# A list schedule of one decoder layer with 112 of its 758 groups of tasks at another rank

## The chip, the cores and the metric

One NeuronCore of a Trainium2 chip. The metric is the device time of one execution in microseconds (us). Every time in this document is that of the device or of the hardware profiler's trace.

## What is computed

One layer of a hybrid decoder on 512 tokens of width 1024, in float32. The reference, cut to what matters here:

```python
ada = c @ w_ada + b_ada                       # six vectors of 1024: sh1, sc1, gt1, sh2, sc2, gt2
h = rms_norm(x, norm1_w) * (1 + sc1) + sh1
proj = h @ w_in                               # 1024 x 10016
att_in, rwkv_in, gate_in = split(proj, ...)   # 4608, 3360, 2048 columns
y_att = attention_mixer(att_in) @ w_att_out   # 3 groups (window, dilation), 8 heads of 64
y_rwkv = rwkv7_mixer(rwkv_in, ...) @ w_rwkv_out   # 16 heads of 64, low-rank decay, a and gate
g_att, g_rwkv = split(sigmoid(gate_in + b_gate))
x = x + gt1 * ((g_att * y_att + g_rwkv * y_rwkv) @ w_o)
h = rms_norm(x, norm2_w) * (1 + sc2) + sh2
x = x + gt2 * conv_ffn(h, w_up, conv_w, conv_b, w_down)   # gated, causal convolution of width 3
return rms_norm(x, norm_f_w)
```

## The kernel before

**Arithmetic.** A long product is made of three matmuls per 128 rows of the contraction: each float32 operand is split into a high part (`hi`, fp32r, by ScalarE) and a low part (`lo`, by VectorE), and hi\*hi, hi\*lo and lo\*hi are added up in one PSUM bank. So every weight block is loaded by a DMA from SP's queue, cast on ScalarE (`whi`, L1181), subtracted on VectorE (`wlo`, L1184) and used by TensorE 24 times (L148). Such a block with its product is a "body". The buffers are few: two raw weight blocks, two split ones, and two PSUM banks (`mm`) for the long products.

**Stages.** The start (conditioning): x is loaded, normed and turned; VectorE multiplies the rows of `w_ada` by c and adds them up in four rounds (L506 and L508), and each round gives two of the eight blocks of h. As the blocks come, the first products of the attention run: four accumulations `early` (e = 0 to 3, over k = 0 to 7) and the value products `v`. The fourth of the `early` ones and the value products sit in `mm` banks; `early` is copied out by ScalarE (e = 0, 1) and VectorE (e = 2, 3, L606). When all of the start is done, a point named `wide` frees its memory for the rest of the attention. Then the attention: the projections `qk00` to `qk12` (part, group), scores `sc`, `stat` (L825), `exp`, turns `pt` and `pts`, values `po`, and at the end the shares of the groups (`pa`, L1067). Then RWKV: three lora products (`lw`, and `lg` twice), and for each of eight pairs of heads the products k, r and v with their token shift. `shift` is one ScalarE instruction (L1192) and one on VectorE (L1194), and the second one releases the `mm` bank. Four groups of two pairs each get the inverse of a triangular matrix (VectorE steps, `inv0` to `inv3`) and a chain of eight steps (`xy`, `u`, `w`, `xo`). Products of the branch gates (`gate`, tile `pg`) fill TensorE beside the chains. At the end of RWKV the products with `w_att_out` (`pa`) and the first ones with `w_rwkv_out` (`pr`) begin.

**What sets the order.** All of this up to the first `pr` products is not written in its final order. `Layer` adds some thousands of tasks to a `Plan`: each has an engine (`PE`, `DVE`, `ACT`, `POOL` or `DMA`, which is SP's queue), an assumed time, a function that writes its instructions, tasks that it depends on, buffers that it takes and gives, and a rank `prio`. `Plan.run` plays through the tasks with the assumed times. Whenever an engine is free, it sorts its ready tasks by `(prio, uid)` and starts the first whose buffers are free. The order in which it starts them is the order of each engine's instructions in the program, and on the chip each engine's queue runs in that order, with semaphores between the queues. The assumed times set the order and nothing else. A lower rank goes first; at equal ranks the task that was added first goes first.

The ranks before follow a few constants: chains 0.0 (`C_`), what empties PSUM 1.0 (`E_`), small matmuls 1.0 and up (`S_`), weight loads and splits 2.0 plus the number of the body (`W_`), long matmuls 10.0 plus that number (`U_`), the preparation of pair m 200.0 + 0.1 m (`V_`), the inverses 200.25, 200.35, 200.65 and 200.75, and 220.0 for what has time (`M_`). The norms and gates of the chains of groups 0 to 2 have 150.0.

**Behind the plan** the rest is written out by hand: the other `pr` products, `w_o` (tile `o`), the up projections (`u`), the down projections (`o`) and the last norm. It begins at about 740 us of the profile.

The change touches one function, `Plan.run`, and adds a table beside it.

Of the kernel before, what the change touches and what calls it, by code (L numbers as in the profile page):

```python
# [43 lines left out]
        self.left, self.at, self.users, self.uid = 0, 0.0, [], 0  # L44


class Plan:


# [18 lines left out]
    def run(self):  # L68
        now, events, busy, open_ = 0.0, [], {}, {}
        room = self.room  # L70

        def push(at, kind, t):
            heapq.heappush(events, (at, kind, t.uid, t))

        for t in self.tasks:
            if not t.left:
                push(0.0, 1, t)
        done = 0
        while events:
            now = events[0][0]  # L80
            while events and events[0][0] <= now + 1e-9:
                _, kind, _, t = heapq.heappop(events)
                if kind == 1:
                    open_.setdefault(t.eng, []).append(t)
                    continue
                if kind == 0:
                    busy[t.eng] = False
                    if t.lag:
                        push(now + t.lag, 2, t)
                        continue  # L90
                for r in t.give:
                    room[r] += 1
                done += 1
                for u in t.users:
                    u.at = max(u.at, now + (self.HOP if u.eng != t.eng and "NO" not in (u.eng, t.eng) else 0.0))
                    u.left -= 1
                    if not u.left:
                        push(u.at, 1, u)
            for eng, ready in open_.items():
                if busy.get(eng):  # L100
                    continue
                ready.sort(key=lambda t: (t.prio, t.uid))
                for t in ready:
                    need = {r: t.take.count(r) for r in t.take}
                    if all(room[r] >= n for r, n in need.items()):
                        for r in t.take:
                            room[r] -= 1
                        ready.remove(t)
                        busy[eng] = True
                        t.fn()  # L110
                        push(now + t.us, 0, t)
                        break
        assert done == len(self.tasks), (now, room, [(t.eng, t.name or t.fn.__qualname__, t.take)
                                                     for r in open_.values() for t in r][:20])
# [2337 lines left out]
```

## Time and profile before

| | us |
|---|---|
| device time, three runs: median | 1192.46 |
| lowest and highest of them | 1192.05, 1192.62 |
| span of the profiled execution, first to last instruction | 1189.3 |
| TensorE busy in it (matmuls) | 1154.6 |
| VectorE busy | 741.6 |
| ScalarE busy | 542.4 |
| GpSimd busy | 130.6 |

The profiled execution is told by its span; 3.16 us lie between that span and the median of the three runs. TensorE shows as busy from the start of a matmul to its modelled end, and ends overlap the next start, so 512-column matmuls of 390 to 400 ns each follow each other every 0.23 us. The idle time before an instruction stands in square brackets in the timeline, with what released it. The DMA engines moved 138.93 MB. The mean granted clock of TensorE over the span is 0.994 of full speed.

### The profile page before, as it was taken

How to read it: one execution, taken by the hardware profiler on the slowest of the kernel's cores; microseconds unless marked ns; L12 is line 12 of the kernel's file. 1: busy time of each engine (PE TensorE's matmuls, PEld its weight loads, DVE VectorE, ACT ScalarE, POOL GpSimd, SP SyncE). 2: the span in 40 equal slices, each digit the busy share in tenths (PEclk: the TensorE clock that was granted, in tenths of full speed). 3: DMA queues.
4: the chain of work that ended last, by engine and by line, in shares of the span. 5: the costliest groups of instructions: out<-in, count | busy, mean ns of one | idle time of the engine just before them, and what ended most of it. 6: DMA issues, size and time to landing. Idle time of an engine off the chain costs nothing.

```text
span 1189.3 us, 19029 instructions
## 1 busy us (share of the span) xinstructions
PE 1154.6 (97%) x7440; PEld 928.5 (78%) x7440; DVE 741.6 (62%) x1250; ACT 542.4 (46%) x1012; POOL 130.6 (11%) x271
## 2 busy tenths in 40 slices
PE   4899999999999999999999999999999999999997
PEld 3788888788687876777787667788888888888886
DVE  6788864432778977756896655845665656562235
ACT  4475622523566374464545543534444444431223
POOL 4000000000300024131103231014000000000001
PEclk9899999999999999999999999999999999999999
DMA  9845873120233332322331626730333333333231
GB/s 315 269 125 168 260 246 108 56 79 1 74 111 89 93 107 85 107 81 85 89 94 48 197 68 190 207 129 19 89 100 95 96 100 94 101 106 106 89 124 71
DMA packets 168329, 138.93 MB, mean 117 GB/s; under 512 B 8785, under 2 KB 150187, under 8 KB 168239
## 3 DMA queue, kind: packets, MB, share of 16 engines
q1 hardware_dynamic: 168095, 137.45, 37.9%
q8 instruction: 58, 0.95, 0.3%
q14 instruction: 32, 0.26, 0.1%
q10 hardware_dynamic: 144, 0.26, 0.1%
HBM read 127.39 MB, written 10.30 MB: 116 GB/s over the span
## 4 chain that ended last, share of the span: by engine, by line
PE 87%; DVE 9%; issue 2%; ACT 1%; DMA 1%; SPq 0%; POOL 0%; POOLq 0%; DVEq 0%; ACTq 0%
PE u L148 22%; PE o L148 13%; PE qk L148 10%; PE v L148 9%; PE pg L148 7%; PE pr L148 3%; PE r L148 3%; PE k L148 3%; PE pa L148 2%; PE pt L151 2%; PE xy L148 2%; PE sc L148 2%; PE early L148 2%; PE po L148 1%; DVE acc L508 1%
## 5 line engine op out<-in xcount | busy, mean ns | idle before, releaser
L194 DVE TENSOR_TENSOR wlo<-raw,whi 128x1024 fp32r<-128x1024 f32 x65 | 79.6, 1225 | 132.9 <-ACT whi L193 132.9
L148 PE MATMUL u<-h2hi,whi 128*128 128x512 f32 (+2 forms) x368 | 140.6, 382 | 0.0
L148 PE MATMUL u<-h2lo,whi 128*128 128x512 f32 (+2 forms) x368 | 140.6, 382 | 0.0
L148 PE MATMUL u<-h2hi,wlo 128*128 128x512 f32 (+2 forms) x368 | 140.5, 382 | 0.0
L1181 ACT CAST whi<-raw 128x1024 fp32r<-128x1024 f32 (+2 forms) x73 | 72.6, 994 | 123.0 <-PE qk L148 47.1
L193 ACT CAST whi<-raw 128x1024 fp32r<-128x1024 f32 x65 | 68.5, 1054 | 90.5 <-PE o L148 53.7
L1184 DVE TENSOR_TENSOR wlo<-raw,whi 128x1024 fp32r<-128x1024 f32 (+2 forms) x73 | 83.8, 1148 | 25.2 <-ACT whi L1181 24.9
L148 PEld LDWEIGHTS u<-h2lo,whi 128*128 128x128 f32 x368 | 69.1, 188 | 13.3 <-POOL h2lo L405 0.2
L148 PEld LDWEIGHTS u<-h2hi,wlo 128*128 128x128 f32 x368 | 69.1, 188 | 13.2
L148 PEld LDWEIGHTS u<-h2hi,whi 128*128 128x128 f32 x368 | 69.1, 188 | 13.0
L2278 DVE SCALAR_TENSOR_TENSOR u<-u,cols,u 128x511 f32<-128x511 f32 x88 | 65.7, 746 | 4.3 <-ACT u L2276 2.7
L148 PE MATMUL qk<-hhi,wlo 128*128 128x512 f32 x160 | 64.0, 400 | 0.0
L148 PE MATMUL qk<-hhi,whi 128*128 128x512 f32 x160 | 63.9, 400 | 0.0
L148 PE MATMUL qk<-hlo,whi 128*128 128x512 f32 x160 | 63.4, 396 | 0.0
L148 PE MATMUL o<-whi,fhi 128*128 128x512 f32 x144 | 56.1, 390 | 0.3 <-DVE u L2278 0.3
L148 PE MATMUL o<-wlo,fhi 128*128 128x512 f32 x144 | 56.0, 389 | 0.0
L148 PE MATMUL o<-whi,flo 128*128 128x512 f32 x144 | 56.0, 389 | 0.0
L148 PE MATMUL pg<-hlo,whi 128*128 128x512 f32 x128 | 51.9, 406 | 0.0
L148 PE MATMUL pg<-hhi,wlo 128*128 128x512 f32 x128 | 51.9, 406 | 0.0
L148 PE MATMUL pg<-hhi,whi 128*128 128x512 f32 x128 | 51.4, 402 | 0.0
L825 DVE CUSTOM_DVE_ANT_0 sm<-sc,m 128x256 f32<-128x256 f32 (+1 forms) x64 | 23.9, 403 | 38.5 <-PE sc L148 37.0
L347 DVE SCALAR_TENSOR_TENSOR acc<-araw,cols,acc 128x1024 f32<-128x1024 f32 x28 | 35.9, 1281 | 12.4 <-DMA araw<-in_w_ada_dram 12.2
(457 smaller groups left out, 2755.3 us busy)
## 6 DMA issues: line engine op xcount, KB each, us to landing
raw<-in_w_in_dram SPq DMA_DIRECT2D x62, 512.0 KB
raw<-in_w_up_dram SPq DMA_DIRECT2D x44, 512.0 KB
araw<-in_w_ada_dram SPq DMA_DIRECT2D x32, 512.0 KB
raw<-in_w_down_dram SPq DMA_DIRECT2D x22, 512.0 KB
araw<-in_w_ada_dram SPq DMA_DIRECT2D x32, 256.0 KB
wvraw<-in_w_in_dram SPq DMA_DIRECT2D x20, 256.0 KB
raw<-in_w_rwkv_out_dram SPq DMA_DIRECT2D x8, 512.0 KB
raw<-in_w_o_dram SPq DMA_DIRECT2D x8, 512.0 KB
```

Of the source, the lines that this page charges most:

```text
L148: return self.nc.tensor.matmul(out, lhsT, rhs, start=start, stop=stop)
L151: self.nc.tensor.matmul(out, in_, self.ident[: in_.shape[0], : in_.shape[0]], is_transpose=True, start=start, stop=stop,)
L193: self.nc.scalar.copy(hl[0], raw)
L194: (lo_eng or self.nc.vector).tensor_tensor(hl[1], raw, hl[0], op=ALU.subtract)
L347: nc.vector.scalar_tensor_tensor(d["acc"], raw, ck, d["acc"], op0=ALU.mult, op1=ALU.add)
L508: nc.vector.scalar_tensor_tensor(a["acc"], a[k], ck, a["acc"], op0=ALU.mult, op1=ALU.add)
L825: nc.vector.tensor_tensor_reduce(d["sm", h][:, :wd], d["sc"][h][:, :wd], m[:, 256 - wd : 256] if gi == 0 else m[:, :wd], 1.0, 3.0e38, op0= ...
L1181: nc.scalar.copy(d["w"][0], d["raw"])
L1184: nc.vector.tensor_tensor(d["w"][1], d["raw"], d["w"][0], op=ALU.subtract)
L2278: nc.vector.scalar_tensor_tensor(u[:, d:], pu[:, : S - d], ch(c), u[:, d:], op0=ALU.mult, op1=ALU.add)
```

## The change

`Plan.run` adds a number to the rank of each task before it starts. The number is looked up in a table by the task's engine, its name, the name of its function and its old rank, rounded to six places; tasks that agree in all four are one group. 112 of the 758 groups stand in the table, and the others add 0. No task, buffer, tile, dependency or assumed time is changed, and neither is anything behind the plan. Most entries move a group from one of the bands above into another. The diff, with the entries that the prediction speaks of and some of the others:

```diff
+RANKS = {
...
+    ('ACT', '', '<lambda>', 200.75): -172.69,
+    ('ACT', '', 'r_hi', 200.1): -201.6,
+    ('ACT', 'k3 hi', 'hi', 50.0): 170.84,
+    ('ACT', 'lg hi', 'hi', 39.0): -39.96,
+    ('ACT', 'lg hi', 'hi', 40.0): -37.56,
...
+    ('ACT', 'r3 hi', 'hi', 51.0): 213.82,
...
+    ('ACT', 'shift', '<lambda>', 1.0): 44.79,
...
+    ('DMA', 'gate in', '<lambda>', 220.0): -160.27,
...
+    ('DMA', 'qk00', 'load', 5.0): -0.19,
...
+    ('DMA', 'v rows', 'v_load', 2.5): -0.07,
+    ('DMA', 'v rows', 'v_load', 4.5): 2.47,
+    ('DMA', 'v rows', 'v_load', 5.5): 2.54,
...
+    ('DMA', 'x', 'load', 2.0): -12.56,
+    ('DVE', '', '<lambda>', 0.0): -12.01,
+    ('DVE', '', '<lambda>', 1.0): -11.39,
+    ('DVE', '', '<lambda>', 200.0): -189.5,
+    ('DVE', '', '<lambda>', 200.1): -185.09,
+    ('DVE', '', '<lambda>', 200.4): -154.39,
+    ('DVE', '', '<lambda>', 200.6): -200.28,
+    ('DVE', '', 'a_row', 200.7): 398.06,
+    ('DVE', '', 'diagonal', 200.65): -191.64,
...
+    ('DVE', '', 'k_row', 200.4): -179.5,
...
+    ('DVE', '', 'recip', 200.25): -190.54,
+    ('DVE', '', 'scaled', 200.65): -168.89,
+    ('DVE', '', 'turned', 200.65): -129.63,
...
+    ('DVE', 'shift', '<lambda>', 1.0): 74.85,
...
+    ('PE', 'early', '<lambda>', 10.52): 109.59,
+    ('PE', 'early', '<lambda>', 10.71): 9.68,
...
+    ('PE', 'lg', '<lambda>', 47.0): -16.82,
...
+    ('PE', 'v', 'prod', 10.35): 99.31,
+    ('PE', 'v', 'prod', 12.0): -41.25,
...
+    ('PE', 'xy2.1', 'state', 0.0): 47.83,
+    ('PE', 'xy2.6', 'state', 0.0): 221.34,
+}
...
         for t in self.tasks:
+            t.prio += RANKS.get((t.eng, t.name, t.fn.__qualname__.split(".")[-1], round(t.prio, 6)), 0.0)
             if not t.left:
                 push(0.0, 1, t)
```

An `early` rank is 10 + 0.1 k + 0.01 e, so 10.52 is the product of block k = 5 for the third accumulation. `v` at 10.15 to 10.75 are the value products of the first two token blocks, and 12.0 those of the other two.

More of the change, by code (lines that the diff above doesn't have):

```diff
@@ L44, in __init__ @@
         self.left, self.at, self.users, self.uid = 0, 0.0, [], 0
+RANKS = {
+    ('ACT', '', '<lambda>', 1.011): 199.35,
+    ('ACT', '', '<lambda>', 200.3): -175.54,
+    ('ACT', '', '<lambda>', 200.4): -47.1,
+    ('ACT', '', '<lambda>', 200.75): -172.69,
+    ('ACT', '', 'cs_tanh', 1.0): 56.44,
+    ('ACT', '', 'g2_hi', 150.0): -124.16,
+    ('ACT', '', 'l2_hi', 1.0): 85.22,
+    ('ACT', '', 'r_hi', 200.1): -201.6,
+    ('ACT', '', 'square', 150.0): -133.66,
+    ('ACT', '', 'tanh', 1.0): 30.43,
+    ('ACT', 'exp', '<lambda>', 1.02): -87.5,
+    ('ACT', 'gate hi', 'hi', 80.0): -69.26,
+    ('ACT', 'k3 hi', 'hi', 50.0): 170.84,
+    ('ACT', 'lg hi', 'hi', 39.0): -39.96,
+    ('ACT', 'lg hi', 'hi', 40.0): -37.56,
+    ('ACT', 'o', 'out', 1.0): 1.36,
+    ('ACT', 'o', 'out', 1.01): 43.46,
+    ('ACT', 'pts', 'turned', 1.01): 50.97,
+    ('ACT', 'pts', 'turned', 1.03): 8.35,
+    ('ACT', 'qk01 hi', 'hi', 13.0): -14.76,
+    ('ACT', 'qk02 hi', 'hi', 16.0): 20.52,
+    ('ACT', 'qk02 hi', 'hi', 29.0): -71.85,
+    ('ACT', 'qk02 hi', 'hi', 30.0): 99.57,
+    ('ACT', 'qk10 hi', 'hi', 7.0): -19.95,
+    ('ACT', 'r3 hi', 'hi', 51.0): 213.82,
+    ('ACT', 'r4 hi', 'hi', 54.0): -10.78,
+    ('ACT', 'rows hi', 'rows_hi', 2.0): -4.29,
+    ('ACT', 'shift', '<lambda>', 1.0): 44.79,
+    ('DMA', 'ada', 'load', 10.0): -3.01,
+    ('DMA', 'ada', 'load', 26.0): -6.79,
+    ('DMA', 'ada', 'load', 29.0): 40.08,
+    ('DMA', 'gate', 'load', 68.0): 3.19,
+    ('DMA', 'gate', 'load', 72.0): -1.71,
+    ('DMA', 'gate', 'load', 78.0): -6.04,
+    ('DMA', 'gate in', '<lambda>', 220.0): -160.27,
+    ('DMA', 'pa', 'load', 83.0): 8.31,
+    ('DMA', 'pa', 'load', 84.0): -46.44,
+    ('DMA', 'pa', 'load', 86.0): -65.94,
+    ('DMA', 'pa', 'load', 87.0): -57.94,
+    ('DMA', 'pr', 'load', 91.0): -88.34,
+    ('DMA', 'qk00', 'load', 5.0): -0.19,
+    ('DMA', 'qk01', 'load', 26.0): -2.53,
+    ('DMA', 'qk11', 'load', 15.0): 1.83,
+    ('DMA', 'qk11', 'load', 28.0): 3.46,
+    ('DMA', 'v rows', 'v_load', 2.5): -0.07,
+    ('DMA', 'v rows', 'v_load', 4.5): 2.47,
+    ('DMA', 'v rows', 'v_load', 5.5): 2.54,
+    ('DMA', 'v7', 'load', 64.0): 11.01,
+    ('DMA', 'vec', 'load', 11.0): -15.84,
+    ('DMA', 'x', 'load', 2.0): -12.56,
[7 more added lines that the diff above has]
+    ('DVE', '', 'diagonal', 200.65): -191.64,
+    ('DVE', '', 'gated', 150.0): -125.46,
+    ('DVE', '', 'k_row', 200.4): -179.5,
+    ('DVE', '', 'l2_lo', 1.0): 86.12,
+    ('DVE', '', 'recip', 200.25): -190.54,
+    ('DVE', '', 'scaled', 200.65): -168.89,
+    ('DVE', '', 'turned', 200.65): -129.63,
+    ('DVE', '', 'var', 150.0): -148.99,
+    ('DVE', 'ada', 'step', 4.0): -13.44,
+    ('DVE', 'ada', 'step', 5.0): -46.24,
+    ('DVE', 'gate lo', 'lo', 76.0): -88.51,
+    ('DVE', 'qk00 lo', 'lo', 6.0): 152.26,
+    ('DVE', 'qk01 lo', 'lo', 25.0): 2.95,
+    ('DVE', 'scan', '<lambda>', 200.7): -5.62,
+    ('DVE', 'shift', '<lambda>', 1.0): 74.85,
+    ('DVE', 'stat', '<lambda>', 1.0): -8.67,
+    ('DVE', 'vec', '<lambda>', 1.0): -49.27,
+    ('PE', 'ada', 'cols', 1.0): 25.46,
+    ('PE', 'early', '<lambda>', 10.1): 0.01,
+    ('PE', 'early', '<lambda>', 10.12): -0.02,
+    ('PE', 'early', '<lambda>', 10.52): 109.59,
+    ('PE', 'early', '<lambda>', 10.71): 9.68,
+    ('PE', 'gate', '<lambda>', 79.0): -57.33,
+    ('PE', 'lg', '<lambda>', 47.0): -16.82,
+    ('PE', 'pa', '<lambda>', 89.0): -39.2,
+    ('PE', 'pb', 'bonus', 1.5): 470.02,
+    ('PE', 'pe', '<lambda>', 0.5): -39.51,
+    ('PE', 'pn', 'norm', 1.0): 24.65,
+    ('PE', 'pn', 'norm', 1.6): 105.39,
+    ('PE', 'po', '<lambda>', 1.0): 11.76,
+    ('PE', 'po', '<lambda>', 1.02): 21.31,
+    ('PE', 'pr', '<lambda>', 97.0): 49.86,
+    ('PE', 'pt', '<lambda>', 1.2): -36.82,
+    ('PE', 'pt', '<lambda>', 1.4): -28.95,
+    ('PE', 'pt', 'turn', 1.0): -197.76,
+    ('PE', 'pt', 'turn', 1.01): -197.96,
+    ('PE', 'pw', 'rates', 1.0): 4.07,
+    ('PE', 'pw', 'rates', 1.5): 52.51,
+    ('PE', 'qk00', '<lambda>', 13.0): -13.99,
+    ('PE', 'qk01', '<lambda>', 34.0): 11.45,
+    ('PE', 'qk02', '<lambda>', 37.0): -34.86,
+    ('PE', 'qk10', '<lambda>', 15.0): -17.55,
+    ('PE', 'qk12', '<lambda>', 40.0): 3.85,
+    ('PE', 'r0', '<lambda>', 50.0): -49.28,
+    ('PE', 'r7', '<lambda>', 71.0): 135.93,
+    ('PE', 'sc', 'scores', 1.0): -49.35,
+    ('PE', 'ty', 'turn', 1.0): 55.74,
+    ('PE', 'v', 'prod', 10.15): -12.93,
+    ('PE', 'v', 'prod', 10.35): 99.31,
+    ('PE', 'v', 'prod', 12.0): -41.25,
+    ('PE', 'v0', '<lambda>', 51.0): -47.48,
+    ('PE', 'v12', 'unit', 44.0): -0.67,
+    ('PE', 'v12', 'unit', 45.0): 0.6,
+    ('PE', 'xy2.1', 'state', 0.0): 47.83,
+    ('PE', 'xy2.6', 'state', 0.0): 221.34,
+}
```

## The prediction

> **What bounds the kernel now.** I read the page first, then the table of windows by stage, then the waits of TensorE, and last the timeline at the places that the waits named.
>
> The head of the page, with the row of TensorE and its two rows in 40 slices of 29.7 us:
>
> ```profile
> span 1189.3 us, 19029 instructions
> ...
> PE 1154.6 (97%) x7440; PEld 928.5 (78%) x7440; DVE 741.6 (62%) x1250; ACT 542.4 (46%) x1012; POOL 130.6 (11%) x271
> ...
> PE   4899999999999999999999999999999999999997
> ...
> PEclk9899999999999999999999999999999999999999
> ```
>
> TensorE is the bound: 97% of the span, and no other engine is over 62%. A new rank changes the order of instructions, not their number, so TensorE's own work stays what it is, and all that a new order can give back is time in which TensorE stands still or runs at a lowered clock. There are 1189.3 - 1154.6 = 34.7 us of standing still. The windows say where (columns: window, its length, then busy time with counts of PE, PEld, DVE, ACT, POOL, granted clock, DMA):
>
> ```profile
> 0.00:42.00 42.00, 22.80 (x96) 18.25 (x97) 29.47 (x54) 20.85 (x29) 13.42 (x38) 0.92 1.00 323
> 42.00:330.00 288.00, 285.66 (x1664) 237.24 (x1663) 170.28 (x317) 128.65 (x277) 14.04 (x25) 0.99 0.43 131
> 330.00:640.00 310.00, 307.89 (x2478) 237.64 (x2476) 240.22 (x436) 167.20 (x323) 50.64 (x97) 1.00 0.32 92
> 640.00:770.00 130.00, 126.86 (x1333) 92.72 (x1334) 83.25 (x157) 67.26 (x146) 30.65 (x62) 1.00 0.49 151
> 770.00:1190.00 420.00, 411.42 (x1874) 342.69 (x1872) 218.40 (x289) 158.44 (x237) 21.87 (x49) 0.99 0.30 94
> ```
>
> PE's length less its busy time is 19.20 us in the conditioning, 2.34 in the attention, 2.11 in the first part of RWKV, 3.14 in its end, and 8.58 behind 770 us, where the ranks do not reach. So the ranked part has 26.8 us, 19.2 of them in a start that waits for data. The waits of TensorE in the windows 0 to 42, 42 to 330 and 640 to 770 name the single places (total, times, longest):
>
> ```profile
> PE ada L148 <- DVE acc L508: 5.4, 2, 2.8
> PE tr L151 <- DVE vv L463: 4.9, 1, 4.9
> PE vec L151 <- DMA rows<-in_norm_w_dram: 3.3, 1, 3.3
> ...
> PE r L148 <- DVE lt L1194: 1.4, 1, 1.4
> PE v L148 <- DVE early L606: 0.8, 1, 0.8
> ...
> PE pa L148 <- issue: 1.2, 1, 1.2
> PE pr L148 <- ACT w L2030: 0.5, 2, 0.3
> PE pr L148 <- DVE w L2031: 0.4, 1, 0.4
> ```
>
> **The change part by part.** Every term is a stretch of TensorE's idle time, since whatever moves elsewhere is hidden as long as TensorE has a matmul ready. Lower ranks go first.
>
> Start. The loads of x get rank 2.0 - 12.56 = -10.56, and the three small loads with the column vectors keep 2.0, so x moves ahead of them on SP's queue. The rows of SP, ScalarE and VectorE:
>
> ```profile
> 0.79 0.40 SPq L268 DMA_DIRECT2D rows<-in_c_dram  x1
> ...
> 1.97 1.78 SPq L454 DMA_DIRECT2D xt<-in_x_dram  x4
> 3.79 6.72 SPq L498 DMA_DIRECT2D araw<-in_w_ada_dram  x8
> ...
> 10.15 1.06 ACT L459 ACTIVATE hlo<-xt 128x1024 fp32r<-128x1024 f32 x1 [0.18 <-DMA xt<-in_x_dram]
> ...
> 11.34 0.15 DVE L463 TENSOR_SCALAR vv<-ss 128x1 f32<-128x1 f32 x1 [0.50 <-ACT hlo L459]
> 11.42 0.49 DVE L506 TENSOR_SCALAR acc<-araw,cols 128x512 f32<-128x512 f32 x1
> ```
>
> The four loads of x start 1.97 - 0.79 = 1.18 us sooner. The last tile of x is squared at 10.15, its variance comes at 11.34, and behind that the first product with w_ada at 11.42. That product also needs the first w_ada load, issued at 3.79, and the column vector, and the number of bytes ahead of that load is the same in either order. The last x landed just before 10.15; the next 256 KB at the 323 GB/s of the window 0 to 42 take 0.8 us more, which puts the product at 10.9 at the soonest: a gain of 0.5, at most 1.18. If the small rows, now queued behind 2 MB of x, come later than that, the gain is gone, and a loss up to the same 1.18 could stand. I take -0.5, the value nearest to the row of the last x. The issue of the x loads and of the vectors is the same 3.0 us on SP, and w_ada behind them starts at 3.79 either way.
>
> One weight load of the attention (qk00, rank 5.0 - 0.19) passes the last eight loads of w_ada, and the third and fourth value loads fall back (4.5 to 6.97, 5.5 to 8.04). That is 512 KB in and 256 KB out ahead of those eight, 256 KB net, 0.8 us at the same 323 GB/s. The cover is TensorE's backlog from 37.75 on:
>
> ```profile
> 37.75 0.77 PE L148 MATMUL early<-hhi,whi 128*128 128x512 f32 x1
> ...
> 62.14 1.37 DVE L606 COPY early<-early 128x512 f32<-128x512 f32 x2 [4.94 <-PE early L148]
> ...
> 63.56 0.39 PE L148 MATMUL v<-wv,hhi 128*128 128x256 f32 x1 [0.78 <-DVE early L606]
> ```
>
> TensorE has no wait between 37.75 and the copy at 62, so I cost it at nothing; without the backlog it is +0.8. The 0.78 at 63.56 is the end of the start: the two matmul banks are taken, and the value products wait until the fourth early product is copied out, second in a row of two copies. The ranks move the third early product back (k=5 from 10.52 to 120.11, and its later k hang on it) and the second too (k=7 from 10.71 to 20.39), so the fourth ends first and its copy runs while TensorE still works on the third. That closes the gap: -0.8. The other way, the third now ends last, and everything that waits for the end of the start waits for its copy: half of the 1.37 is 0.7, so +0.7 at the other end. I take -0.8, since the wait named is that on the copy of the fourth.
>
> The gap in the lora stage. The second lora gate sits in a bank, its mix `shift` waits on VectorE behind the eight share products, and the r product has no bank:
>
> ```profile
> 320.13 3.36 DVE L1067 TENSOR_TENSOR o<-o,pw 128x512 f32<-128x512 f32 x5 [0.24 <-PE pw L148]
> 323.41 0.73 DVE L1194 SCALAR_TENSOR_TENSOR lt<-lg,mu,sh 32x512 f32<-32x512 f32 x1
> 324.07 1.20 DVE L1184 TENSOR_TENSOR wlo<-raw,whi 128x1024 fp32r<-128x1024 f32 x1
> ...
> 324.19 0.50 PE L148 MATMUL r<-hhi,whi 128*128 128x512 f32 x1 [1.45 <-DVE lt L1194]
> ...
> 322.00:325.00 3.00, 1.47 (x6) 0.86 (x6) 2.99 (x5) 1.58 (x3) 1.24 (x2) 1.00 0.46 175
> 325.14:328.55 3.41, 3.41 (x10) 2.64 (x9) 2.73 (x4) 2.28 (x4) 3.28 (x3) 0.50 0.26 80
> ```
>
> The gap is 1.45 us, and right behind it the granted clock is 0.50 for 3.41 us, which costs half of that, 1.7 us: 3.15 together. The weight splits of both gates on ScalarE go forward (39.0 to -0.96 and 40.0 to 2.44), and so do the first gate's matmuls (47.0 to 30.18), which may let the gates end ahead of the share products: then -3.15. But `shift` on VectorE goes from 1.0 to 75.85, behind every weight split ranked up to 75 as well as behind the share products. If nothing else moves, the split at 324.07 runs first, and the r product waits 1.2 us more: +1.2. Ends -3.15 and +1.2, nothing in the rows nearer to either; I take 0. [...]
>
> RWKV. Many tasks of pairs 0, 1, 4 and 6 and of the inverses of groups 0, 2 and 3 go from about 200 to mostly between 0 and 71, that is ahead of the late weight splits, so that the groups' chains can begin sooner; single chain steps (`xy2.1`, `xy2.6`) and splits (`k3 hi` to 220.84, `r3 hi` to 264.82) fall back. The idle time that this can reach is 2.11 in 330 to 640 and 3.14 in 640 to 770, less the 0.9 before the last pr products, which are written behind the plan: 4.3 us. One of these waits, the 1.2 put down to issue, waits for nothing that the profile shows. I take half of 4.3, -2.1, with the ends 0 and -4.3 for old gaps; new gaps are a rival below.
>
> Unseen in busy time is what it costs to break up a row of long matmuls with small ones. The timeline near 661 us:
>
> ```profile
> 660.76 0.40 PE L148 MATMUL pg<-hhi,whi 128*128 128x512 f32 x1
> 661.00 0.39 PE L148 MATMUL pg<-hlo,whi 128*128 128x512 f32 x1
> 661.32 0.45 PE L148 MATMUL u<-uv,bkt 128*64 128x64 f32 x8
> ```
>
> From long to long it is 661.00 - 660.76 = 0.24, from long to small 0.32: 0.08 for each entry. A new order makes some entries more or fewer; twenty of them would be 1.6 us, so -1.6 to +1.6, and 0 taken, for nothing in the ranks says which way.
>
> Sum: -0.5 - 0.8 + 0 - 2.1 + 0 = -3.4 us, a span of 1185.9. The profiled span lies 3.16 us below the median of the three runs, 1192.46, and I carry that difference over: 1192.46 - 3.4 = 1189.1 us. What a measurement of this kernel can tell from no change is about 0.2%, 2.4 us.
>
> **The rivals.** First, the gaps move and do not shrink: where TensorE waits for a bank or a split, some other task is now the late one. For it speaks that the attention has only two waits in 288 us, so there is nothing to win there, and that a rank acts only where two tasks are ready at once. Against it, that two named gaps are touched directly. The start's -0.5 and the -0.8 would be eaten by one new wait of the 1.4 size: 1192.5 us.
>
> Second, the lora gap closes as well, with the halved clock behind it: -3.4 - 3.15 = -6.5, or 1185.9 us. For it the two gates' forward ranks, against it the rank of `shift`.
>
> Third, slower: the late `shift`. It runs 27 times and each time releases one of the two banks that feed all long products. For it speaks the row at 324.07: a split costs 1.2 us, and behind a short wait the clock fell to 0.50 at a price of 1.7. Against it, VectorE is busy 240.22 of 310 us, so it often has room, and a bank has the length of a whole other product, 24 matmuls at 0.24, 5.8 us, before it is missed. It decides where `shift` is held more than 5.8 us less its own 0.73 and ScalarE's share before it, about 4 us, or three splits and the pair's tasks in a row. Each such place then costs 1.2 to 2.9 us; two of them with the clock and one without give 2 x 2.9 + 1.2 = 7.0, which together with -0.5 and -0.8 is +5.7: 1198.2 us.
>
> **How the numbers follow.** Forecast as summed 0.42, gaps that move 0.30, lora gap closed 0.09, slower by `shift` 0.19. The likeliest gives 1189.1; its own terms (start -1.18 to 0, copy -0.8 to +0.7, RWKV -4.3 to 0) reach 1186.2 to 1193.2. For eight in ten I go down past the second rival by the entries' 1.6, to 1184, and up close to the third, to 1197. Faster by over 0.2% holds most of the forecast (0.37 of 0.42), the closed gap 0.09 and a little of the first rival: 0.49. Slower is the third and a part of the first: 0.21. Same 0.30.
>
> **What would show it.** In the profile after: the four x loads ahead of the vector rows, and the first w_ada product near 10.9 instead of 11.42; no wait of the value products on the copies of the early products; idle time of TensorE in 330 to 770 near 3 us instead of 5.25; the wait of r on `shift` still about 1.4 us with a stretch of clock at 0.50 behind it. Wrong would be: waits of the k, r or v products on `shift` at several places, a second slice with a clock under 1.00 between 80 and 760 us, a wider wait at the end of the start, or a stage after 770 us that is not the same length as before.

## Result: 9.8 us faster, 6.5 us more than forecast

| | before | after |
|---|---|---|
| device time, median of five runs each on one chip (us) | 1192.46 | 1182.64 |
| lowest and highest | 1190.37, 1193.17 | 1179.73, 1183.43 |
| ratio with 95% interval | | 0.9907 [0.9896, 0.9918] |
| span of the profiled execution | 1189.3 | 1180.9 |
| device time of that execution | | 1182.64 |

The forecast was 1189.1, with a range of 1184 to 1197. The time fell below the range. The head of the page after, with TensorE's rows in 40 slices:

```profile
span 1180.9 us, 19029 instructions
...
PE 1149.8 (97%) x7440; PEld 927.5 (79%) x7440; DVE 742.9 (63%) x1250; ACT 543.7 (46%) x1012; POOL 130.2 (11%) x271
...
PE   4999999999999999999999999999999999999997
PEclk9999999999999999999999999999999999999999
```

The instructions are the same 19029. TensorE's busy time falls by 4.8 us although it does the same 7440 matmuls. One at half clock shows as busy for longer (0.73 us in a row of 53.59 further down, 0.40 at full clock), and the second slice of the clock, an 8 before, is a 9 now; the stretches below show that this is not all of it.

Windows at fixed times mislead once the work inside them has moved, so I cut both executions at the same four matmuls instead: the first projection of the attention, the first k product, the last r product of the first pair, and the first mix with `w_o`, which stands behind the plan. Their rows before (first four) and after:

```profile
69.42 0.40 PE L148 MATMUL qk<-hhi,whi 128*128 128x512 f32 x1
314.41 0.40 PE L148 MATMUL k<-hhi,whi 128*128 128x512 f32 x1
331.16 0.39 PE L148 MATMUL r<-hhi,wlo 128*128 128x512 f32 x1
771.17 0.39 PE L148 MATMUL o<-wohi,mhi 128*128 128x512 f32 x1
```

```profile
67.75 0.40 PE L265 MATMUL qk<-hhi,whi 128*128 128x512 f32 x1
312.48 0.40 PE L265 MATMUL k<-hhi,whi 128*128 128x512 f32 x1
325.14 0.39 PE L265 MATMUL r<-hhi,wlo 128*128 128x512 f32 x1
762.80 0.39 PE L265 MATMUL o<-wohi,mhi 128*128 128x512 f32 x1
```

That gives a ledger of stretches in us, which I use for every kernel below:

| stretch | before | after | difference | forecast |
|---|---|---|---|---|
| start, to the first `qk` | 69.42 | 67.75 | -1.67 | -1.3 |
| attention, to the first `k` | 244.99 | 244.73 | -0.26 | 0 |
| lora, to the last r of pair 0 | 16.75 | 12.66 | -4.09 | 0 |
| RWKV, to the first `w_o` product | 440.01 | 437.66 | -2.35 | -2.1 |
| behind the plan | 418.13 | 418.13 | 0.00 | 0 |

The sum is -8.37, against -3.4 forecast. The same cut as windows shows what the differences are made of. Attention, lora and RWKV, before and then after (columns as in the prediction):

```profile
69.42:314.41 244.99, 244.99 (x1449) 203.21 (x1448) 140.78 (x274) 109.27 (x250) 7.42 (x20) 1.00 0.43 129
314.41:331.16 16.75, 15.22 (x61) 11.66 (x59) 12.91 (x18) 6.39 (x9) 6.62 (x5) 0.90 0.40 124
331.16:771.17 440.01, 434.76 (x3810) 330.36 (x3809) 324.63 (x594) 234.64 (x470) 81.29 (x159) 1.00 0.37 108
```

```profile
67.75:312.48 244.73, 244.73 (x1457) 204.62 (x1455) 143.01 (x278) 109.38 (x251) 9.23 (x20) 1.00 0.44 130
312.48:325.14 12.66, 12.16 (x53) 9.68 (x52) 12.08 (x13) 4.96 (x7) 6.65 (x5) 1.00 0.37 126
325.14:762.80 437.66, 432.99 (x3810) 330.28 (x3809) 325.78 (x599) 238.87 (x473) 78.08 (x159) 1.00 0.38 110
```

The length of a stretch less TensorE's busy time is idle time. It is 0 in the attention both times, falls from 1.53 to 0.50 in lora and from 5.25 to 4.67 in RWKV, and from 20.0 to 18.1 in the start: 3.5 us of the 8.37. For RWKV's 5.25 the forecast had been about 3. Another 2.9 is half of the 5.78 us of matmuls that ran at half clock from 35.01 to 41.83 before; the 3.41 us at half clock behind the r product have a counterpart after, behind the new stall in the start. The remaining 2 us are neither: in the attention and in RWKV the matmuls follow each other more closely, and the start loses some of that again. The cuts lie at fixed matmuls and others cross them: lora has 53 instead of 61 and the attention 1457 instead of 1449, so about 1 us of lora's -4.09 (three share products and four small ones, at their spacing) is work that has moved into the attention.

The waits of TensorE after, in the windows 0 to 42, 42 to 330 and 330 to 640 (total, times, longest):

```profile
PE vec L268 <- DMA rows<-in_b_ada_dram: 9.4, 1, 9.4
PE ada L265 <- DVE acc L625: 2.9, 1, 2.9
...
PE early L265 <- ACT whi L675: 1.1, 1, 1.1
PE early L265 <- DVE wlo L678: 0.8, 1, 0.8
PE r L265 <- DVE lt L1311: 0.5, 1, 0.5
...
PE pe L265 <- DVE lt L1688: 0.3, 1, 0.3
PE pe L265 <- DVE lt L1729: 0.3, 1, 0.3
```

The second wait on the sums of `w_ada` is gone (5.4 in two before, 2.9 in one now), the wait of the value products on the copy (0.8) is gone, a new stall of 1.1 + 0.8 us stands in the early products, and the r product waits 0.5 instead of 1.4. The wait of 9.4 for a vector row stands where 3.3 for a row and 4.9 for x's variance stood before, since x now goes ahead of the rows.

### The profile page after: what moved, and what is told of

The parts are those of the page before. It is cut to its first block, busy times and chain, and to the rows that moved or that the text cites. A ratio compares the mean times of both kernels' runs of the same rounds, so it can differ in the third digit from the quotient of the medians.

```text
span 1180.9 us, 19029 instructions
## 1 busy us (share of the span) xinstructions
PE 1149.8 (97%) x7440; PEld 927.5 (79%) x7440; DVE 742.9 (63%) x1250; ACT 543.7 (46%) x1012; POOL 130.2 (11%) x271
## 4 chain that ended last, share of the span: by engine, by line
PE 90%; DVE 5%; ACT 2%; issue 1%; DMA 1%; SPq 0%; POOL 0%; POOLq 0%; DVEq 0%; ACTq 0%
PE u L265 23%; PE o L265 13%; PE qk L265 9%; PE v L265 9%; PE pg L265 7%; PE k L265 4%; PE pr L265 3%; PE r L265 3%; PE pa L265 2%; PE pt L268 2%; PE xy L265 2%; PE early L265 2%; PE sc L265 2%; PE po L265 1%; PE xo L265 1%
## 5 line engine op out<-in xcount | busy, mean ns | idle before, releaser
L2147 ACT CAST fhi<-u 128x512 fp32r<-128x512 f32 x22 | 13.7, 621 | 60.8 <-DVE u L2406 60.8
```

Of the source, the lines that this page charges most:

```text
L2147: self.nc.scalar.copy(hi, src)
```

## The experiments

Each kernel is the kernel before with a part of the table. I split the 112 entries into four groups: 13 of the start, 39 of the attention (with three of the lora gates: the weight splits of both on ScalarE and the matmuls of the first), 2 of `shift` (ScalarE's and VectorE's), and the other 58, of RWKV. Medians are from rounds beside the kernel before, whose median in them was 1192.46 to 1193.21. The stretches are those of each kernel's profiled execution; behind the plan all have 418.1 to 418.2, but for `e8_early_back` with 418.5. One execution is a small base. The four kernels that keep TensorE's order in the start (`e4_shift`, `e5_rwkv_shift`, `e10_gates`, `e14_rwkv`) read 69.10 to 70.89 there against 69.42; six with the changed kernel's order read 64.74 to 65.83, and two, the changed kernel's first profile and `e3_start_att_shift`, 67.75 and 67.86 with a halved clock near 53 us. RWKV in one and the same order differs by 0.3 to 0.5 us between two executions.

| kernel | median | ratio to before | start | attention | lora | RWKV |
|---|---|---|---|---|---|---|
| before | 1192.46 | | 69.42 | 244.99 | 16.75 | 440.01 |
| `e6_x` | 1192.03 | 0.9999 [0.9991, 1.0008] | 68.42 | 245.25 | 16.78 | 442.35 |
| `e9_v_rows` | 1188.64 | 0.9970 [0.9960, 0.9979] | 65.46 | 244.82 | 16.74 | 440.51 |
| `e1_start` | 1189.08 | 0.9971 [0.9957, 0.9984] | 65.08 | 245.72 | 16.76 | 440.12 |
| `e2_start_att` | 1186.48 | 0.9947 [0.9929, 0.9966] | 65.83 | 245.06 | 12.89 | 441.79 |
| `e3_start_att_shift` | 1184.40 | 0.9928 [0.9911, 0.9944] | 67.86 | 244.70 | 15.00 | 438.40 |
| `e4_shift` | 1196.59 | 1.0030 [1.0019, 1.0041] | 69.50 | 245.99 | 21.05 | 439.23 |
| `e5_rwkv_shift` | 1193.14 | 1.0003 [0.9993, 1.0013] | 69.10 | 246.16 | 20.18 | 437.05 |
| `e14_rwkv` | 1191.40 | 0.9987 [0.9978, 0.9996] | 70.89 | 244.84 | 15.12 | 439.94 |
| `e10_gates` | 1210.82 | 1.0138 [1.0124, 1.0152] | 69.91 | 242.52 | 14.29 | 464.45 |
| `e11_start_att_no_gates` | 1193.22 | 0.9996 [0.9987, 1.0006] | 65.41 | 245.58 | 11.98 | 451.97 |
| `e15_all_but_gates` | 1184.23 | 0.9933 [0.9920, 0.9947] | 65.61 | 244.71 | 15.57 | 437.43 |
| `e13_no_shift` | 1183.32 | 0.9921 [0.9908, 0.9933] | 64.79 | 245.40 | 11.68 | 440.50 |
| `e7_shift_dve_back` | 1182.00 | 0.9898 [0.9885, 0.9912] | 65.21 | 245.65 | 11.88 | 438.91 |
| `e16_after_again` | 1180.70 | 0.9898 [0.9884, 0.9911] | 64.74 | 244.93 | 12.67 | 437.97 |
| `e8_early_back` | 1179.14 | 0.9894 [0.9876, 0.9912] | 64.68 | 248.45 | 12.66 | 438.13 |
| `e12_both_back` | 1179.40 | 0.9871 [0.9856, 0.9887] | 63.71 | 247.37 | 11.90 | 440.04 |

### The groups, one on top of the other

The start alone, with its entries:

```diff
+    ('ACT', 'rows hi', 'rows_hi', 2.0): -4.29,
+    ('DMA', 'qk00', 'load', 5.0): -0.19,
+    ('DMA', 'v rows', 'v_load', 2.5): -0.07,
+    ('DMA', 'v rows', 'v_load', 4.5): 2.47,
+    ('DMA', 'v rows', 'v_load', 5.5): 2.54,
+    ('DMA', 'x', 'load', 2.0): -12.56,
+    ('PE', 'early', '<lambda>', 10.1): 0.01,
+    ('PE', 'early', '<lambda>', 10.12): -0.02,
+    ('PE', 'early', '<lambda>', 10.52): 109.59,
+    ('PE', 'early', '<lambda>', 10.71): 9.68,
+    ('PE', 'v', 'prod', 10.15): -12.93,
+    ('PE', 'v', 'prod', 10.35): 99.31,
+    ('PE', 'v', 'prod', 12.0): -41.25,
```

> Only the 13 entries that move tasks of the start (loads of x, value rows and qk00, the cast of the rows, the early and value products). Theory A, the gain is a sum of separate stretches: TensorE's first qk product came 1.67 us sooner in the changed kernel, so this gives -1.7 us against before, and the wait of r on shift stays 1.4 us with a stretch of clock at 0.50 behind it. Theory B, the ranks work only together: the order of the start alone is swallowed at the next bank or buffer, and the time is within 0.7 us of before.

Measured: 3.4 us faster in the medians, 4.3 in the start stretch, more than either theory had, and the r product still waits 1.4 us. Then the attention's entries on top:

```diff
+    ('ACT', 'exp', '<lambda>', 1.02): -87.5,
+    ('ACT', 'lg hi', 'hi', 39.0): -39.96,
+    ('ACT', 'lg hi', 'hi', 40.0): -37.56,
...
+    ('PE', 'lg', '<lambda>', 47.0): -16.82,
+    ('PE', 'po', '<lambda>', 1.0): 11.76,
...
+    ('PE', 'qk02', '<lambda>', 37.0): -34.86,
+    ('PE', 'qk12', '<lambda>', 40.0): 3.85,
+    ('PE', 'sc', 'scores', 1.0): -49.35,
...
```

> The 13 entries of the start and the 39 of the attention and the lora gates; those of shift and RWKV are left out. Theory A: between the first k product and the last matmul of r0 the changed kernel gained another 4.1 us, and the attention's ranks do it, because they end the attention about 7 us sooner and so spread the share products on VectorE: -1.7 - 4.1 = -5.8 us, the wait of r on shift under 0.5 us and no clock under 1.00 near it. Theory B: closing that gap needs the ranks of r0, v0 and shift too, and this gives -2 us, with the gap still there.

Another 2.6 us in the medians, 6.0 in all, as the first theory had it: the lora stretch falls from 16.76 to 12.89, RWKV rises by 1.7. So the lora gap, for which I had put 0, is closed by the attention's group, the gates' three entries included. Then `shift` on top:

```diff
+    ('ACT', 'shift', '<lambda>', 1.0): 44.79,
+    ('DVE', 'shift', '<lambda>', 1.0): 74.85,
```

> As the run with the start and the attention, with the two entries of shift added (ScalarE 1.0 to 45.79, VectorE 1.0 to 75.85). The rival that the late shift costs banks: +1.2 us or more against the run without them, and waits of k, r or v on shift. Theory A: in RWKV a split already stood ahead of most shifts, so the two kernels are within 0.6 us of each other. Theory B: the entries were found together and shift frees ScalarE and VectorE for others: another -1 to -2 us.

The median falls by another 2.1, near the last theory, though the intervals of the two overlap. The stretches show a trade: lora +2.1, RWKV -3.4. The start of this execution is longer by 2.0, with a halved clock from 53.65 to 57.07 that the profile of `e2_start_att` does not have.

### Shift alone, and RWKV alone and with it

The two `shift` entries by themselves:

```diff
+    ('ACT', 'shift', '<lambda>', 1.0): 44.79,
+    ('DVE', 'shift', '<lambda>', 1.0): 74.85,
```

> The two entries of shift alone in the kernel before. The rival of the prediction: the r product waits for the split as well, 1.45 + 1.2 = 2.65 us, with the halved clock behind it as before, and further waits on shift: +1.2 to +5 us. Theory A: only that one place changes: +1.2 us. Theory B: nothing, within 0.6 us.

Slower by 4.1 us. VectorE and the first r product in this kernel's timeline, and the window at half clock around them:

```profile
320.96 2.78 DVE L1074 TENSOR_TENSOR o<-o,pw 128x512 f32<-128x512 f32 x4 [0.52 <-PE pw L155]
323.67 2.25 DVE L1191 TENSOR_TENSOR wlo<-raw,whi 128x1024 fp32r<-128x1024 f32 x1
325.84 2.03 DVE L1215 TENSOR_TENSOR sg0l<-lt,sg0h 128x512 fp32r<-128x512 f32 x1
327.91 0.74 DVE L1201 SCALAR_TENSOR_TENSOR lt<-lg,mu,sh 32x512 f32<-32x512 f32 x1
328.70 0.80 PE L155 MATMUL r<-hhi,whi 128*128 128x512 f32 x1 [5.68 <-DVE lt L1201]
```

```profile
325.29:332.11 6.82, 3.41 (x8) 2.73 (x9) 4.97 (x6) 3.01 (x5) 3.50 (x3) 0.50 0.63 200
```

Two instructions of VectorE (2.25 and 2.03 us) now run ahead of the `shift`, TensorE stands still for 5.68 us, and the granted clock is 0.50 for 6.82. This is the mechanism of my third rival, at one place and not at several. In RWKV the same two entries bring 0.8, little more than two executions of one order can differ.

The RWKV entries together with `shift`:

```diff
+    ('ACT', '', 'r_hi', 200.1): -201.6,
...
+    ('ACT', 'shift', '<lambda>', 1.0): 44.79,
...
+    ('DVE', '', 'recip', 200.25): -190.54,
...
+    ('DVE', 'shift', '<lambda>', 1.0): 74.85,
...
+    ('PE', 'xy2.6', 'state', 0.0): 221.34,
```

> The 58 entries of RWKV and the end and the two of shift, without start and attention. Theory A (separate stretches): RWKV's -2 us together with the +4.1 us that shift alone cost: +2 us. Theory B (the ranks fit each other): r0 and v0 and the others give the bank to something else while shift waits, and the wait of r on shift stays under 3 us: -1 to -3 us.

No change in the time, which neither theory had: lora +3.4, RWKV -3.0. And without `shift`:

```diff
+    ('ACT', '', 'r_hi', 200.1): -201.6,
...
+    ('DVE', '', 'recip', 200.25): -190.54,
...
+    ('PE', 'xy2.6', 'state', 0.0): 221.34,
```

> The 58 RWKV entries alone, on the kernel before. Theory (the term of RWKV stands by itself, about -2.1 as forecast, and is worked off after the first r product): the wait of 1.4 us and the halved clock at 325 stay, 1192.5 - 2.1 = 1190.4 us, within 1. Rival (as with the gates, the entries fit only the order that the others make): 1192.5 or slower, with new waits in 640 to 770.

The stretch of RWKV is 439.94 against 440.01 in this execution, so the preparation of the pairs and the inverses bring nothing there that shows. It is made up differently, though: TensorE's busy time is 1.5 us shorter (433.25 against 434.76) and its idle time 1.4 longer (6.69 against 5.25); with `shift` as well, in `e5_rwkv_shift`, the idle time is 4.67. The execution has the wait of 1.4 us before the r product but no halved clock behind it, which is where its lora stretch of 15.12 comes from. The median is 1.8 us under that of the kernel before in its rounds (1193.21), and the interval, 0.9978 to 0.9996, stands for 0.5 to 2.6 us. The theory's 2.1 lies within that, but not in the stretch that it named, so where this gain comes from stays open.

### What closes the lora gap

The gates' three entries alone (the expectation calls them those of the second gate; 40.0 is the second gate's split, 39.0 and 47.0 are the first gate's split and matmuls):

```diff
+    ('ACT', 'lg hi', 'hi', 39.0): -39.96,
+    ('ACT', 'lg hi', 'hi', 40.0): -37.56,
+    ('PE', 'lg', '<lambda>', 47.0): -16.82,
```

> The kernel before with only the three entries of the second lora gate (two weight splits on ScalarE, its matmuls). Theory (the gap before the first r product closed because the attention, and with it VectorE's share products, ended sooner; the gates' own ranks did not close it): r still waits about 1.4 us on VectorE's shift, with the clock at 0.50 for 3.41 us behind it, and the time is 1192.5, within 1.5 of the kernel before. Rival (the gates' ranks closed it, as my second rival had it): no wait of r on the shift, and 1192.5 - 3.15 = 1189.3 us.

Both expectations missed: 17.6 us slower. The wait of r on the `shift` is gone, as my second rival had it, and lora falls to 14.29. But RWKV rises by 24.4. The longest of its waits behind 330 us, and two windows of it (the granted clock is the number ahead of the DMA share):

```profile
PE v L156 <- DVE k L1202: 5.4, 1, 5.4
```

```profile
349.91:360.15 10.24, 5.41 (x15) 4.34 (x16) 6.56 (x11) 4.20 (x8) 0.60 (x2) 0.50 0.25 66
640.00:770.00 130.00, 120.78 (x1374) 85.49 (x1373) 75.27 (x156) 61.69 (x152) 32.67 (x67) 0.95 0.38 118
```

Three ranks at 300 us leave TensorE idle for 9.2 us of the 130 at the end of RWKV, and around the wait of 5.4 us the clock is at half for 10.24 us, 5.41 of them with matmuls. Then `e2_start_att` without these three:

```diff
-    ('ACT', 'lg hi', 'hi', 39.0): -39.96,
-    ('ACT', 'lg hi', 'hi', 40.0): -37.56,
-    ('PE', 'lg', '<lambda>', 47.0): -16.82,
```

> The start and attention entries, without the three of the lora gates. Theory (the attention's earlier end closed the gap): no wait of r on the shift over 0.5 us and no halved clock behind it, 1186.5 us as with the gates, within 1. Rival (the gates closed it): the wait of 1.4 us and the 3.41 us of halved clock are back, and the time is that of the start entries alone, 1189.1 us, within 1.

The lora stretch is 11.98 with no wait of r: the attention's other entries close the gap without the gates. The time was missed by both expectations, because RWKV is 451.97, that is 10.2 longer than with the gates. So in this company the three entries are worth 6 to 7 us (by the ratios and by the medians), but none of it at the gap.

The whole table without the three:

```diff
 RANKS = {
-    ('ACT', 'lg hi', 'hi', 39.0): -39.96,
-    ('ACT', 'lg hi', 'hi', 40.0): -37.56,
-    ('PE', 'lg', '<lambda>', 47.0): -16.82,
```

> The changed kernel without the three entries of the lora gates. Theory (what the missing gates cost in the earlier run, 6.7 us, came from the end of RWKV running dry, and the RWKV entries do not mend that): 1182.6 + 4 to 7 = 1187 to 1190 us, with over 6 us of idle TensorE time in 640 to 770. Rival (the RWKV entries make the end of RWKV independent of the gates' order): 1183 us, within 1.5, with idle time there near 3.6.

3.5 us slower than the changed kernel on the same chip. RWKV is 437.43, so with the RWKV entries and the late `shift` it does not need the gates' entries, and the rival holds there. The loss is at the lora gap, one line of this kernel's waits:

```profile
PE r L262 <- DVE lt L1308: 3.5, 1, 3.5
```

The `shift` of the gate starts 254.10 us behind the first `qk` here (319.71 - 65.61) and 251.26 behind it in the changed kernel (319.01 - 67.75).

### Is the late shift worth having

The changed kernel without VectorE's entry, and without both:

```diff
 RANKS = {
-    ('DVE', 'shift', '<lambda>', 1.0): 74.85,
```

> The changed kernel without the late rank of the shift on VectorE (ScalarE's half of it stays late). Theory (with the share products early, the late shift costs only the wait of 0.5 us that is left on the r product, and gives nothing in the chains): that wait is gone and the time is 1182.64 - 0.5 = 1182.1, within 1. Rival (the late shift on VectorE lets splits and the inverses pass and is what brought 2.1 us with the start and attention entries): 1184.7 us, with new waits in 330 to 770.

```diff
 RANKS = {
-    ('ACT', 'shift', '<lambda>', 1.0): 44.79,
-    ('DVE', 'shift', '<lambda>', 1.0): 74.85,
```

> The changed kernel without both entries of the shift. Theory (with the share products early the late shift neither costs nor brings more than the 0.5 us wait of the first r product): 1182.1 us, within 1, and no wait of r on the shift. Rival (the late shift brings the 2.1 us that it brought with the start and attention entries): 1184.7 us.

Without VectorE's entry 1182.0, the same as the changed kernel: lora is 0.8 shorter, RWKV 0.9 to 1.3 longer, which nearly cancels. Without both 1183.32, 2.6 above the changed kernel on that chip (ratios 0.9921 [0.9908, 0.9933] and 0.9898 [0.9884, 0.9911], which just overlap), so nearer to the rival. Lora is 1.0 shorter, RWKV 2.5 longer, nearly all of it idle time (7.00 us against 4.67 and, in the second profile, 4.96). Two waits of this kernel in 330 to 640 are not in the changed one:

```profile
PE v L263 <- ACT gs L2153: 1.0, 1, 1.0
PE pg L263 <- ACT na L1450: 0.8, 1, 0.8
```

Both are waits for ScalarE. Neither stands in `e7_shift_dve_back`, which keeps ScalarE's late rank, so they come and go with ScalarE's entry. That its early `shift` stands before `gs` and `na` is my reading.

### The start

The loads of x alone, and one value load alone:

```diff
+    ('DMA', 'x', 'load', 2.0): -12.56,
```

> One entry alone in the kernel before: the four loads of x ahead of the vector rows. The prediction's step: the first product with w_ada at 10.9 instead of 11.42, and -0.5 us (at most -1.2) at the end. Theory B, x makes the start's gain: -2.5 us or more. Theory C: VectorE's order absorbs it, within 0.4 us, with the wait at 36 us still there.

```diff
+    ('DMA', 'v rows', 'v_load', 2.5): -0.07,
```

> One entry alone in the kernel before: the first load of value rows goes ahead of the first load of weight rows (2.5 to 2.43). Theory A, the start's gain is VectorE's: in the run of the start alone the subtraction of the value rows fell into VectorE's idle time at 16.3 us, and that of the second weight rows then ran at 26.9 instead of 35.8, so TensorE's 2.79 us wait at 36.05 and the halved clock behind it (about 2 us of the matmuls from 37.75 on) vanish: -2.5 to -4 us. Theory B, the loads of x make the start's gain: less than 0.7 us from this.

The x loads change nothing in the time that the ratio can show (0.9999, give or take 1 us), and both waits on the sums are still there. The value load, with its step of 0.07 past the first weight rows (one block in two loads), brings 3.9 us, as much as all 13 entries, as the first theory had it. VectorE and the long wait in the timeline before, then VectorE in the timeline with the one entry, and the waits there:

```profile
28.16 0.69 DVE L574 TENSOR_TENSOR wv<-wvraw,wv 128x512 fp32r<-128x512 f32 x1
35.83 1.22 DVE L561 TENSOR_TENSOR wlo<-raw,whi 128x1024 fp32r<-128x1024 f32 x1
36.05 1.84 PE L148 MATMUL ada<-few,acc 128*128 128x1 f32 x8 [2.79 <-DVE acc L508]
```

```profile
27.90 1.22 DVE L567 TENSOR_TENSOR wlo<-raw,whi 128x1024 fp32r<-128x1024 f32 x1
```

```profile
PE ada L154 <- DVE acc L514: 2.6, 1, 2.6
```

Before, VectorE splits the value rows at 28.16 and comes to the second weight rows at 35.83; with the load order turned it splits them at 27.90, and of the two waits on the sums one is left. The early products of these rows can then run while the third round is summed, and where TensorE stood for 2.79 us before 36.05, with the clock at half from 35.01 to 41.83, it has work.

Then the changed kernel without the entry that moves back the third early product, and without it and VectorE's `shift`:

```diff
 RANKS = {
-    ('PE', 'early', '<lambda>', 10.52): 109.59,
```

> The changed kernel without one entry: the third early product at k = 5 keeps 10.52. Theory A: that entry made the new wait at 52 us (1.13 and 0.76 us, with the clock at 0.50 behind it in the profile), because the third weight rows' buffer is held until that product is done; without it that wait goes, and the wait of the value products on the copy (0.78 us) comes back: -1 to -3 us against the changed kernel, 1180 to 1181.5. Theory B, the prediction's: the entry closes the wait on the copy and is worth 0.8 us: +0.8, 1183.4.

```diff
 RANKS = {
-    ('DVE', 'shift', '<lambda>', 1.0): 74.85,
-    ('PE', 'early', '<lambda>', 10.52): 109.59,
```

> The changed kernel without the late rank of the third early product (k = 5) and without that of the shift on VectorE. Theory (the two are independent; the first put a stall of 1.9 us and a halved clock at 52 us into the start): 1179.1 - 0.5 = 1178.6 us, within 1. Rival (the 3.5 us of the first are a matter of where gaps fall in the clock's windows, not of the stall): between 1180.5 and 1182.6.

The first has no stall near 52 us and, still, no wait of the value products on the copies; 1179.14 us. The second, 1179.4, has the lowest ratio of all kernels, 0.9871 [0.9856, 0.9887]. Both have a median below the changed kernel's 1182.64 and 1180.7, but only the second's interval is clear of the first of these two measurements, and it meets the second, so a gain over the changed kernel is likely and not settled. So for `e8_early_back` the first theory is right about the stall and wrong about the wait on the copy, which stays away. Their longer attention stretches come with waits for `stat` of 1.4 and 0.8 us and with the clock at half for 3.4 us near 210. The one is not right behind the other, as `e8_early_back` shows; the first window is the 3.41 us ahead of the halved clock:

```profile
197.25 1.05 PE L264 MATMUL sc<-qk,qk 64*128 64x128 f32 x8 [1.35 <-DVE stat L941]
...
207.91:211.32 3.41, 3.41 (x36) 3.17 (x32) 3.02 (x10) 2.61 (x7) 0.00 (x0) 1.00 0.02 5
211.32:214.73 3.41, 3.41 (x28) 2.56 (x26) 1.73 (x5) 1.96 (x6) 0.00 (x0) 0.50 0.57 154
```

The wait ends 14 us before the clock falls, and TensorE has no idle time in the window between. What halved the clock there stays open.

### The changed kernel once more

The table is the changed kernel's own, on the chip of `e13_no_shift`, `e14_rwkv` and `e15_all_but_gates`.

> The changed kernel once more, on the chip of the three others: 1182.6 us, within 1, with the stall of early products near 52 us; its profile shows whether a halved clock follows it this time.

1180.7, which is 1.9 under the expectation. The stall in the timeline of the first profile of the changed kernel and a window behind it, then both in this one:

```profile
51.24 1.04 ACT L675 CAST whi<-raw 128x1024 fp32r<-128x1024 f32 x1 [2.64 <-PE early L265]
52.33 0.50 PE L265 MATMUL early<-hhi,whi 128*128 128x512 f32 x1 [1.13 <-ACT whi L675]
53.59 0.73 PE L265 MATMUL early<-hhi,wlo 128*128 128x512 f32 x1 [0.76 <-DVE wlo L678]
```

```profile
53.69:57.10 3.41, 3.41 (x8) 2.65 (x9) 1.24 (x2) 0.44 (x1) 0.00 (x0) 0.50 0.26 47
```

```profile
50.91 0.50 PE L265 MATMUL early<-hhi,whi 128*128 128x512 f32 x1 [1.13 <-ACT whi L675]
52.17 0.50 PE L265 MATMUL early<-hhi,wlo 128*128 128x512 f32 x1 [0.76 <-DVE wlo L678]
```

```profile
50.50:54.50 4.00, 2.83 (x11) 2.14 (x12) 2.52 (x3) 2.18 (x4) 0.00 (x0) 1.00 0.07 25
```

The gaps are equal to the hundredth, 1.13 and 0.76 us; once the clock is at 0.50 for 3.41 us behind them, costing 1.7, and once it stays at 1.00. With it the start is 67.75, without it 64.74. Seven more kernels have the same stall in their profiles (1.13 or 1.14, and 0.76); only `e3_start_att_shift` has a halved clock behind it.

## Why the prediction was wrong

**What was right.** TensorE stayed the bound, its matmuls and the 418.1 us behind the plan did not change (the 8.58 us of idle time that I read there include 0.7 behind the end of the execution), and most of the gain came out of idle time (3.5 us) and halved clock (2.9). That nothing else could be gained was wrong by the 2 us of matmuls that follow each other more closely. The value products no longer wait for the copies. The first `w_ada` product starts earlier, as the timeline after shows, at 10.51 instead of 11.42 where I had said 10.9 at the soonest:

```profile
10.51 0.49 DVE L623 TENSOR_SCALAR acc<-araw,cols 128x512 f32<-128x512 f32 x1
```

**Start: the sum near by luck, its terms wrong.** I gave x -0.5 and the copy -0.8. For x alone the ratio leaves room for 1 us either way; its start stretch of 68.42 lies below the 69.10 to 70.89 of the kernels that keep the order, so -0.5 is not refuted. Measured are -3.9 for a value load that I did not cost at all. I had named only the two value loads that fall back, and took VectorE's order as given; a load that comes earlier makes a split ready earlier and changes what VectorE picks next. The 19.2 us of idle time in the start were seen, and the row with 5.4 us in two waits was quoted, but no step asked which entry touches it. Also wrong was the reason for the copy: the wait is gone without the third product's late rank (`e8_early_back`), and that rank makes the new stall of 1.9 us: in the row of 51.24 ScalarE's split waited 2.64 us for an early product, by my reading the third one, which now holds its split buffer longer. The stretch of -1.67, near my -1.3, is -4.68 in the second profile of the same kernel, and five other kernels with that order read 64.79 to 65.83, near the second profile's 64.74. Of the 3.0 between the two profiles, 1.7 is the clock behind the stall, 0.56 the first early product (at 22.09 and 21.53), and the other 0.86 is lost right behind that product: the early products start 0.43 us apart until 26.46 in the first profile and until 24.12 in the second, and 0.23 apart from there on.

**Lora: the step that failed.** I put 0 between ends of -3.15 and +1.2, because the late `shift` stood against the early gates. Measured is -4.09, the largest part of the miss. I judged the two groups that name the tile and not what the `shift` waits for. The last share products on VectorE stand in the row of 320.13 before; after:

```profile
313.38 2.78 DVE L1184 TENSOR_TENSOR o<-o,pw 128x512 f32<-128x512 f32 x4 [0.23 <-PE pw L265]
316.39 0.69 DVE L1184 TENSOR_TENSOR o<-o,pw 128x512 f32<-128x512 f32 x1 [0.24 <-PE pw L265]
317.00 2.09 DVE L1301 TENSOR_TENSOR wlo<-raw,whi 128x1024 fp32r<-128x1024 f32 x1
319.01 0.73 DVE L1311 SCALAR_TENSOR_TENSOR lt<-lg,mu,sh 32x512 f32<-32x512 f32 x1
319.80 0.50 PE L265 MATMUL r<-hhi,whi 128*128 128x512 f32 x1 [0.49 <-DVE lt L1311]
```

The split does run ahead of the `shift`, as I said, and it even takes 2.09 us. But the shares end at 317.1 instead of 323.5, so the wait is 0.49 and no halved clock follows. The attention, which I had written off with "there is nothing to win there", does its tail in another order: its last scores start at 296.94 instead of 303.12 and its last values at 303.69 instead of 310.75, while the last projection (276.41 instead of 259.66) and the first lora product `lw` (its last matmul at 305.59 instead of 294.48) go back. Counted from the first `qk`, which itself starts 1.67 us sooner, the scores are 4.5 and the values 5.4 us ahead. The shares hang on the values, and the `shift` stood behind the shares. The company decides: the late `shift` costs 4.3 us in this stretch by itself, 2.1 with start and attention, 1.0 with all. Of the 4.09, 1.7 is the halved clock and 0.96 the wait, which is what closing the gap was priced at, 3.15, less the 0.49 that is left. Most of the other 1.4 is the work that crossed the cut into the attention, and the attention did not grow by it.

**RWKV: the size right by luck, the cause wrong.** -2.1 forecast, -2.35 and -2.04 in the two profiles. I derived it as idle time, from the preparation of pairs and inverses. Idle time gave 0.58 of the 2.35; the other 1.77 is the same 3810 matmuls in less busy time. The RWKV entries alone gave -0.07, and the whole table without `shift` 440.50, a loss of 0.5. The gain needs the late `shift`, which I had as the cause of the slower case: it takes the stretch down by 2.5 to 3.4 us in three companies (`e2_start_att` to `e3_start_att_shift`, `e14_rwkv` to `e5_rwkv_shift`, `e13_no_shift` to `e16_after_again`). Breaking up rows of long matmuls, for which I took 0, is where the busy time points: in the attention a `qk` product is followed by a value product 12 times before and 3 times after, 0.35 and 0.32 us from start to start where `qk` follows `qk` in 0.23. No run tests that term by itself, so its share stays open.

**The offset.** I carried over 3.16 us between the span and the median. The profiled execution after took 1182.64 with a span of 1180.9, and the difference is 1.7 to 1.8 in all executions on record. So the one profiled execution before, whose device time is not on record, lay about 1.4 us below the median, and that was not to be added to the kernel after. With the stretches' -4.97 this makes the miss of -6.46: -4.97 - 1.45, and 0.04 of rounding.

**The rivals.** The second (gap closed, 1185.9) was nearest, with chance 0.09. Its cause, the gates, closes the gap alone (`e10_gates`, at a loss elsewhere) and is needed beside the late `shift` (3.5 us of waiting without them), but start and attention close the gap without the gates. The first shows in the start's new stall of 1.9 us, which did not eat the gain. The third is real where `shift` is alone.

## What to carry to other kernels

When ranks change, go through what each costly wait is queued behind, not through the entries that name its tile: one of the two large gains here came from scores and values that end about 5 us sooner a stage before the wait, and the other from one value load that goes ahead of two weight loads. Do not price groups of ranks one by one; the same three entries were worth +17.6, about -6 and -3.5 us in three companies. And carry a change of span over to a median only with the time of the same execution beside the span.

## What the chip showed that I had not expected

A gap of TensorE of 1.45 us, the one before the r product in the kernel before, had the clock at 0.50 right behind it for 3.41 us, and equal gaps need not have that behind them: 1.13 + 0.76 us gave 3.41 us at 0.50 in one execution of the changed kernel and none in another (in two of the nine profiles that have this stall), and the 1.4 or 1.5 us before the r product had it in four kernels but not in `e14_rwkv`. Nor need a gap stand right ahead: in `e8_early_back` TensorE had no idle time in the 3.41 us before the clock fell. The stretches at half clock in the rows here are 3.41 us or two or three times that (6.82 in `e4_shift`, 10.24 in `e10_gates`). In the profile before, the granted clock goes to 0.50 at 35.01 and 325.14 and back to 1.00 at 41.83 and 328.55: these changes lie 6.82, 283.31 and 3.41 us apart, which is 2, 83 and 1 times one length. Of the 3.41 us ahead of the two falls TensorE was idle for 2.06 and 1.53 us, and for 1.89 ahead of the one at 53.69 in the profile after. Whether the place of a gap among such stretches decides what it costs, as the rival of `e12_both_back` has it, was not shown, so why equal gaps cost 1.7 us or nothing stays open. The five runs of the changed kernel, 1179.73 with a granted clock of 0.999 and 1182.1 to 1183.43 with 0.996 or 0.997, differ by 2.4 to 3.7 us, one to two times 1.7. So at 0.2% a gap's price is a chance and not a number.
